# Row arithmetic and weight pieces move between GpSimd, VectorE and ACT in a two-block fp32 kernel

## The chip, the cores and the metric

The kernel runs on one core of one Trainium2 chip. The metric is the device time of one execution in microseconds (us). Its engines are TensorE (PE; PEld is its weight load), VectorE (DVE), ScalarE (ACT), GpSimd (POOL) and SyncE (SP), which issues most of the DMA loads.

## The reference, cut to what matters

The input is 256 tokens of width 1024. A first block (latent attention and retention side by side, then a feed-forward layer) is followed by a second (a hybrid of a delta rule and stick-breaking attention, then a mixture of 32 experts). All is fp32.

```python
# first block
h = x * (1.0 + sc1) + sh1                      # six modulation rows from c
proj = h @ w_in                                # latent attention + retention inputs
y = concat([mla(...), retention(...)]) @ w_out
x = layer_norm(ALPHA * x + gt1 * y, ln1_g, ln1_b)
h = x * (1.0 + sc2) + sh2
f = square(relu(h @ w_ff1)) @ w_ff2            # width 4096
x = layer_norm(ALPHA * x + gt2 * f, ln2_g, ln2_b)
# second block: 16 meta tokens in front, then
proj = x @ w_in                                # delta rule q, k, v; gates; attention q, k, v
dn_qkv = silu(causal_depthwise_conv(dn_qkv, conv_w))   # four taps
merged = gate0 * (o_dn @ w_branch_dn) + gate1 * (o_sb @ w_branch_sb)
x = layer_norm(ALPHA * x + merged @ w_out, ...)
x = layer_norm(ALPHA * x + moe(x), ...)        # router, then 32 experts
```

Where the text says residual rows, it means ALPHA * x with the layer norm's gain g and offset b of the layer before folded in: ALPHA * (x * g + b), two rows of 1024 numbers on all 128 partitions.

## The kernel before, in words

The 256 tokens are two tiles of 128 (xh[0] and xh[1], 128x1024 each). Weights come in slabs of 1 MB from SP's queue into a ring of three buffers (tile `raw`). A matrix product in fp32 is made of three products of rounded parts (`mm3`, L317 to L319): high by high, low by high, high by low. So each slab is cut in pieces of 128x1024 by `piece`: ACT casts the high part (`hi`, L299), then VectorE, or GpSimd where the caller says so, subtracts it from the slab to get the low part (`lo`, L300). A pair of buffers for such a piece is free again when TensorE has used it; there are four pairs, and one more (`wx`) until the feed-forward's end.

A list scheduler puts the instructions of each engine in order; `issue_after(x)` forbids it to put one ahead of x. Each engine then runs its own list in order, and semaphores join the lists.

The stages, in order of time: modulation and input projection; `first_mixers`, in which attention heads (`mla`) run interleaved with retention and with pieces of the modulation (`ada`); in it the softmax's scale is L654, its exponential L658, the next heads' q and k projections follow; `residuals` (L811 to L816) is a generator that loads two rows, lets ACT scale them by ALPHA, and lets GpSimd multiply and add them to both tiles; the output projection; `feed_forward`, whose loop of 16 turns computes f (L317 to L319, tile `f`), ffr (ACT, relu), ffs (DVE, the square, L894), its high and low parts ffh (L470) and ffl (L471), and one turn later the second product (tile `ff`). At its end `split` cuts four pieces of the second block's weights, the residual's sum (L874, L875) and the layer norm run per token tile, and a diagonal matrix of reciprocal deviations (L999) turns the normalized tile into fT. `delta_inputs` makes six projections `dn` of two blocks of 128 channels each, copies them (xp, ACT), applies four taps of the convolution (L1082 the first, L1084 the other three) and silu (L1085), and transposes the result (kT, vT). Then come the mixers, the router and the experts (`moe`), whose slabs stream in as the router's list of experts says (SP, L1917).

Of the kernel before, what the change touches and what calls it, by code (L numbers as in the profile page):

```python
# [44 lines left out]
SPLITS = 4  # L45
# [173 lines left out]
class Core:  # L219
# [70 lines left out]
    def piece(self, parts, t, i, size, pool):  # L290
# [5 lines left out]
        wp, bufs = (self.wx, 1) if self.wx and self.cuts % (SPLITS + 1) == 0 else (self.wp, SPLITS)  # L296
# [248 lines left out]
    def first_mixers(self, qc, krp, rr, sg, res):  # L545
# [52 lines left out]
        for i in range(NH // 2 + 2):  # L598
            for j in (i, i - 1, i - 2):
                if 0 <= j < NH // 2:  # L600
# [4 lines left out]
                    if i:  # L605
                        next(ret, None)
            if i == 1:
# [7 lines left out]
        with self.tc.issue_after(self.copied):  # L615
            next(res)
# [4 lines left out]
    def mla(self, i, uq, ukv, ch, cl, kr, vt):  # L621
# [13 lines left out]
        for j, (no, ro) in enumerate(((lo, hi), (hi, lo))):  # L635
# [3 lines left out]
            self.copied = nc.gpsimd.tensor_copy(kk[ro, j, :], kr[ro]).ins  # L639
# [22 lines left out]
        for j in range(2):  # L662
            for t, c in enumerate((slice(0, P), slice(P, 3 * P))):
                e = 2 * j + t
                nc.vector.tensor_scalar(p[:, j, c], p[:, j, c], r[:, e:e + 1], None, op0=ALU.mult)
# [141 lines left out]
    def residuals(self, row, xh, ring=None):  # L807
# [3 lines left out]
        nc.scalar.mul(g, g, ALPHA)  # L811
        nc.scalar.mul(b, b, ALPHA)
        yield
        for x in xh:
            nc.gpsimd.tensor_tensor(x, x, g, op=ALU.mult)
            nc.gpsimd.tensor_tensor(x, x, b, op=ALU.add)  # L816
        yield
# [59 lines left out]
    def feed_forward(self, gt2):  # L877
# [34 lines left out]
        for i in range(nf):  # L912
            last = first(i)
            if i == 2:
                res = self.xh
                for _ in self.residuals(2, res):
                    pass
# [15 lines left out]
        def split(after=None):  # L933
            i, j = next(cut)
            with self.tc.issue_after(after) if after else nullcontext():
                self.piece(parts[i], raw[i], j, 2048, True)
# [13 lines left out]
        split()  # L950
        for t in range(2):
# [10 lines left out]
            last = self.spread(rs[:, 0:1], res[t], s[:, 2:3])  # L962
            split(last)
            nc.vector.scalar_tensor_tensor(x2, x2, rs[:, 0:1], b2, op0=ALU.mult, op1=ALU.add, accum_out=s[:, 3:4])
            nc.vector.tensor_scalar(s[:, 4:5], s[:, 3:4], -1.0 / D, None, op0=ALU.mult)
            nc.vector.scalar_tensor_tensor(xh[t], x2, s[:, 4:5], ge, op0=ALU.add, op1=ALU.mult)
            self.spread(self.re[:, t:t + 1], x2, s[:, 4:5])
            diag[t], last = self.diagonal(self.re[:, t:t + 1])
            if t == 0:
                split(last)  # L970
# [85 lines left out]
    def delta_inputs(self, chains):  # L1056
# [10 lines left out]
        for i in range(6):  # L1067
            pd = [self.ps("dn") for _ in range(2)]
            for last in self.products(self.weights2(256 * i, (1,)), [p[:, :TM] for p in pd]):
# [7 lines left out]
            for b in range(2):  # L1077
# [4 lines left out]
                nc.vector.tensor_scalar(y, xp[:, b, :TM], tap(0), None, op0=ALU.mult)  # L1082
# [386 lines left out]
    def second_mixers(self):  # L1469
# [27 lines left out]
        for t in range(2):  # L1497
            r = self.small()[:, 0:1]
            nc.vector.tensor_scalar(r, self.re[:, t:t + 1], ALPHA, None, op0=ALU.mult)
            nc.scalar.mul(self.xh[t], self.xh[t], r)  # L1500
            nc.gpsimd.tensor_tensor(self.xh[t], self.xh[t], b, op=ALU.add)
# [58 lines left out]
    def mix_out(self):  # L1560
# [27 lines left out]
        def norm(t):  # L1588
            mean, r = self.stats(res[t], out=self.rs[:, 6 + t:7 + t])
            nc.vector.tensor_scalar(res[t], res[t], mean, r, op0=ALU.subtract, op1=ALU.mult)  # L1590

        between = {(1, 0, 3): [(turn, 0, 0)], (1, 1, 2): [(turn, 0, 1), (norm, 0)],
                   (1, 1, 3): [(logits, 0, 0), (logits, 0, 1), (self.choose, 0, pl[0]), (turn, 1, 0)]}
# [182 lines left out]
    def moe(self, xh, pl):  # L1776
# [6 lines left out]
        low(nc.gpsimd, 0, slice(0, D))  # L1783
# [376 lines left out]
```

## Time and profile before

| | before |
|---|---|
| time, median of 3 runs | 917.5 us (914.66 to 918.17) |
| the profiled execution | 914.81 us |
| its span, first to last instruction | 913.1 us |
| mean granted clock of TensorE | 0.957 |
| TensorE busy | 812.8 us, 89% |
| VectorE busy | 511.7 us, 56% |
| ACT busy | 310.4 us, 34% |
| GpSimd busy | 117.2 us, 13% |

Shares are means over stages that differ: a stage's own waits tell what a change in it is worth. In a row of the order of time the bracket gives how long the engine was idle ahead of the instruction and what ended that. A row with "x2" is two instructions that follow each other directly.

### The profile page before, as it was taken

Reading aid. Unit: us, or ns where it says so; the run is one execution under the profiler, and the core shown is the slowest. Engines: PE = TensorE matmul, PEld = TensorE weight load, DVE = VectorE, ACT = ScalarE, POOL = GpSimd, SP = SyncE. Lnnn points to the kernel's source line nnn. Section 1 sums busy time; section 2 is a strip of 40 time slices with the busy share of each in tenths; the row PEclk is TensorE's granted clock in tenths of the full one; section 3 lists DMA queues with packets and bytes.
Section 4 is the critical chain, followed back from the end, with each engine's and each line's share of the span. In section 5 each row is a group of like instructions: output and inputs, shape, how many; then the busy total and the mean of one; then the engine's idle time right before and its main releaser. Section 6 shows DMA issues by size and latency. Waiting matters only on the chain.

```text
span 913.1 us, 13514 instructions
## 1 busy us (share of the span) xinstructions
PE 812.8 (89%) x5311; PEld 611.3 (67%) x5311; DVE 511.7 (56%) x971; ACT 310.4 (34%) x491; POOL 117.2 (13%) x121
## 2 busy tenths in 40 slices
PE   4989789989999999889798999999988988866884
PEld 3886456668999998679797997899863443322321
DVE  4595748595655555845787458875655333120214
ACT  3343336354444444333463343544332211100101
POOL 0002400140000001452415201300010000000000
PEclk9999989989999999797999999999979999999987
DMA  8967546655755555033332130489655999999994
GB/s 310 365 230 299 209 185 253 232 192 180 254 185 189 185 192 193 24 127 136 136 139 84 42 108 13 145 339 335 264 229 244 421 414 421 421 421 421 422 416 179
DMA packets 35895, 218.10 MB, mean 239 GB/s; under 512 B 5976, under 2 KB 6496, under 8 KB 12144
## 3 DMA queue, kind: packets, MB, share of 16 engines
q1 hardware_dynamic: 33888, 215.09, 61.0%
q10 hardware_dynamic: 1936, 2.07, 0.8%
q8 instruction: 44, 0.72, 0.3%
q14 instruction: 27, 0.22, 0.1%
HBM read 216.09 MB, written 1.05 MB: 238 GB/s over the span
## 4 chain that ended last, share of the span: by engine, by line
PE 62%; DMA 17%; DVE 13%; ACT 4%; POOL 2%; issue 2%; SPq 0%; DVEq 0%; ACTq 0%; POOLq 0%
DMA expert<-in_w_down 8%; DMA raw<-in_w_gu 4%; PE gu L323 4%; PE ff L319 3%; PE ff L317 3%; PE ff L318 3%; PE f L319 3%; PE f L317 3%; PE f L318 3%; DMA expert<-in_w_gu 2%; PE dn L323 2%; PE Z L323 2%; PE xT L323 2%; PE y L318 2%; PE gate L317 2%
## 5 line engine op out<-in xcount | busy, mean ns | idle before, releaser
L300 DVE TENSOR_TENSOR lo<-raw,hi 128x1024 fp32r<-128x1024 f32 (+1 forms) x145 | 175.6, 1224 | 96.1 <-ACT hi L299 95.7
L299 ACT CAST hi<-raw 128x1024 fp32r<-128x1024 f32 (+1 forms) x155 | 156.6, 1028 | 176.7 <-PE ff L319 57.2
L323 PE MATMUL gu<-expert,xT 128*32 128x512 f32 (+1 forms) x424 | 81.4, 629 | 9.5 <-DMA expert<-in_w_gu 9.5
L317 PE MATMUL f<-hTh,hi 128*128 128x256 f32 x256 | 72.1, 282 | 0.0
L319 PE MATMUL f<-hTh,lo 128*128 128x256 f32 x256 | 71.8, 280 | 0.0
L318 PE MATMUL f<-hTl,hi 128*128 128x256 f32 x256 | 71.7, 280 | 0.0
L323 PEld LDWEIGHTS gu<-expert,xT 128*32 128x32 f32 (+1 forms) x424 | 20.0, 122 | 55.8 <-issue 36.4
L317 PE MATMUL ff<-hi,ffh 128*128 128x512 f32 x128 | 52.2, 408 | 4.4 <-DVE ffh L470 4.4
L323 PE MATMUL dn<-expert,aT 128*32 128x512 f32 (+1 forms) x224 | 46.9, 626 | 9.7 <-DMA expert<-in_w_down 9.7
L319 PE MATMUL ff<-hi,ffl 128*128 128x512 f32 x128 | 52.6, 411 | 2.0 <-DVE ffl L471 2.0
L318 PE MATMUL ff<-lo,ffh 128*128 128x512 f32 x128 | 52.2, 408 | 0.0
L318 PEld LDWEIGHTS f<-hTl,hi 128*128 128x128 f32 x256 | 48.2, 188 | 0.9 <-issue 0.2
L317 PEld LDWEIGHTS f<-hTh,hi 128*128 128x128 f32 x256 | 48.2, 188 | 0.9 <-issue 0.2
L319 PEld LDWEIGHTS f<-hTh,lo 128*128 128x128 f32 x256 | 48.3, 189 | 0.0
L2005 DVE TENSOR_TENSOR a<-gu,a 128x256 f32<-128x256 f32 x10 | 4.2, 422 | 72.8 <-ACT a L2004 72.8
L300 POOL TENSOR_TENSOR lo<-raw,hi 128x1024 fp32r<-128x1024 f32 x10 | 25.1, 2518 | 121.3 <-ACT hi L299 121.3
L323 PEld LDWEIGHTS dn<-expert,aT 128*32 128x32 f32 (+1 forms) x224 | 11.3, 121 | 39.4 <-issue 19.3
L317 PE MATMUL gate<-hTh,hi 128*128 128x256 f32 x128 | 37.4, 292 | 0.0
L2027 DVE SCALAR_TENSOR_TENSOR yl<-dn,s,yh 128x512 fp32r<-128x512 f32 x20 | 15.0, 749 | 38.8 <-ACT yh L2026 38.8
L323 PE MATMUL xT<-P,hTh 128*128 128x256 f32 x80 | 25.1, 339 | 12.7 <-ACT xT L1959 11.2
L319 PE MATMUL gate<-hTh,lo 128*128 128x256 f32 x128 | 36.1, 282 | 0.0
L318 PE MATMUL gate<-hTl,hi 128*128 128x256 f32 x128 | 36.0, 281 | 0.0
(597 smaller groups left out, 1981.0 us busy)
## 6 DMA issues: line engine op xcount, KB each, us to landing
expert<-in_w_gu SPq DMA_DIRECT2D x53, 1024.0 KB, 13.7
raw<-in_w_ff SPq DMA_DIRECT2D x32, 1024.0 KB, 4.8
expert<-in_w_down SPq DMA_DIRECT2D x24, 1024.0 KB, 19.7
raw<-in_w_in SPq DMA_DIRECT2D x22, 1024.0 KB, 4.8
raw<-in_w_gu SPq DMA_DIRECT2D x11, 1024.0 KB, 19.3
wa<-in_w_ada SPq DMA_DIRECT2D x8, 1024.0 KB, 8.7
raw<-in_w_gate SPq DMA_DIRECT2D x8, 1024.0 KB, 4.7
raw<-in_w_ada SPq DMA_DIRECT2D x8, 1024.0 KB, 4.8
```

The costliest lines, as they stand in the source:

```text
L299: nc.scalar.copy(h[:, :w], f)
L300: (nc.gpsimd if pool else nc.vector).tensor_tensor(l[:, :w], f, h[:, :w].bitcast(F32), op=ALU.subtract)
L317: mm(out, sh, mh, start=first, stop=False)
L318: mm(out, sh, ml, start=False, stop=False)
L319: return mm(out, sl, mh, start=False, stop=last)
L323: i = self.nc.tensor.matmul(out, lhsT, rhs, start=first, stop=last).ins
L2005: nc.vector.tensor_tensor(a, pg[:, FE:], a, op=ALU.mult)
L2027: nc.vector.scalar_tensor_tensor(yl, py, w[:, 0:1], yh.bitcast(F32), op0=ALU.mult, op1=ALU.subtract)
```

## The change

It has six parts:

1. `residuals` uses two VectorE instructions per tile (x * ALPHA * g, then b * ALPHA + x) in place of two ACT scalings and two GpSimd instructions per tile. In `first_mixers` they are taken one at a time in turns 1 to 4 of the loop; in `feed_forward` the rows are loaded in turn 1, and one instruction follows the f product of each of turns 2 to 5.
2. In `delta_inputs` the second piece of each slab has its low part cut by VectorE, and the first tap goes from VectorE to ACT.
3. The four low parts at the feed-forward's end go from GpSimd to VectorE, two behind the last ffl, two behind the first tile's normalization.
4. Behind the second block's mixers one VectorE instruction takes the place of ACT's multiply and GpSimd's add, for each tile.
5. In `moe` the low part of the first tile goes from GpSimd to VectorE, behind the first tile's choice of experts.
6. While `wx` is open, it has two pairs of buffers, so there are six pairs and not five.

```diff
-SPLITS = 4
+SPLITS, MORE_SPLITS = 4, 2
...
-        wp, bufs = (self.wx, 1) if self.wx and self.cuts % (SPLITS + 1) == 0 else (self.wp, SPLITS)
+        more = self.wx and self.cuts % (SPLITS + MORE_SPLITS) < MORE_SPLITS
+        wp, bufs = (self.wx, MORE_SPLITS) if more else (self.wp, SPLITS)
...
+            if 0 < i <= 4:
+                next(res)
...
-        with self.tc.issue_after(self.copied):
-            next(res)
...
         g, b = self.row(row, "rowg", ring), self.row(row + 1, "rowb", ring)
-        nc.scalar.mul(g, g, ALPHA)
-        nc.scalar.mul(b, b, ALPHA)
         yield
         for x in xh:
-            nc.gpsimd.tensor_tensor(x, x, g, op=ALU.mult)
-            nc.gpsimd.tensor_tensor(x, x, b, op=ALU.add)
-        yield
+            nc.vector.scalar_tensor_tensor(x, x, ALPHA, g, op0=ALU.mult, op1=ALU.mult)
+            yield
+            nc.vector.scalar_tensor_tensor(x, b, ALPHA, x, op0=ALU.mult, op1=ALU.add)
+            yield
...
-            if i == 2:
+            if i == 1:
                 res = self.xh
-                for _ in self.residuals(2, res):
-                    pass
+                rows = self.residuals(2, res)
+                next(rows)
+            if 1 < i < 6:
+                with self.tc.issue_after(last):
+                    next(rows)
...
-                self.piece(parts[i], raw[i], j, 2048, True)
+                self.piece(parts[i], raw[i], j, 2048, False)
...
-        split()
+        for _ in range(2):
+            split(last)
...
-            last = self.spread(rs[:, 0:1], res[t], s[:, 2:3])
-            split(last)
+            self.spread(rs[:, 0:1], res[t], s[:, 2:3])
...
-            nc.vector.scalar_tensor_tensor(xh[t], x2, s[:, 4:5], ge, op0=ALU.add, op1=ALU.mult)
+            last = nc.vector.scalar_tensor_tensor(xh[t], x2, s[:, 4:5], ge, op0=ALU.add, op1=ALU.mult).ins
...
             if t == 0:
-                split(last)
+                for _ in range(2):
+                    split(last)
...
-            for last in self.products(self.weights2(256 * i, (1,)), [p[:, :TM] for p in pd]):
+            for last in self.products(self.weights2(256 * i), [p[:, :TM] for p in pd]):
...
-                nc.vector.tensor_scalar(y, xp[:, b, :TM], tap(0), None, op0=ALU.mult)
+                nc.scalar.mul(y, xp[:, b, :TM], tap(0))
...
-            nc.scalar.mul(self.xh[t], self.xh[t], r)
-            nc.gpsimd.tensor_tensor(self.xh[t], self.xh[t], b, op=ALU.add)
+            nc.vector.scalar_tensor_tensor(self.xh[t], self.xh[t], r, b, op0=ALU.mult, op1=ALU.add)
...
-        low(nc.gpsimd, 0, slice(0, D))
+        with self.tc.issue_after(self.last):
+            low(nc.vector, 0, slice(0, D))
```

What it does to the order is shown at three places. On VectorE in attention, ahead of the scale of the latent queries (`s` from `ss`), the list before was:

```order
L300 TENSOR_TENSOR lo_836<-raw_833,hi_835 128x1024
L300 TENSOR_TENSOR lo_840<-raw_833,hi_839 128x1024
L300 TENSOR_TENSOR lo_846<-raw_843,hi_845 128x1024
L578 TENSOR_SCALAR s_119_858<-ss_851 128x2 x2
L582 TENSOR_TENSOR rmsd_862<-ident,s_119_858 128x512
```

The same place after, where xh_100 and xh_101 are the two token tiles:

```order
L301 TENSOR_TENSOR lo_838<-raw_831,hi_837 128x1024
L301 TENSOR_TENSOR lo_844<-raw_841,hi_843 128x1024
L814 SCALAR_TENSOR_TENSOR xh_100<-xh_100,rowg_750 128x1024
L814 SCALAR_TENSOR_TENSOR xh_101<-xh_101,rowg_750 128x1024
L816 SCALAR_TENSOR_TENSOR xh_100<-rowb_752,xh_100 128x1024
L816 SCALAR_TENSOR_TENSOR xh_101<-rowb_752,xh_101 128x1024
L579 TENSOR_SCALAR s_119_856<-ss_849 128x2 x2
L583 TENSOR_TENSOR rmsd_860<-ident,s_119_856 128x512
```

Four instructions of 128x1024 now stand between the last low part and the scale. On ACT at the feed-forward's end, before (hi is a cast of a piece, sq the square of a token tile):

```order
L299 CAST hi_3246<-raw_3240 128x1024
L299 CAST hi_3272<-raw_3258 128x1024
L892 ACTIVATE ffr_3222<-f_460_3173 128x512
L372 ACTIVATE sq_3312,s_488_3311<-xh_100,s_483_3300 128x1024
L299 CAST hi_3316<-raw_3258 128x1024
L299 CAST hi_3330<-raw_3260 128x1024
L372 ACTIVATE sq_3324,s_491_3323<-x_3308,s_483_3300 128x1024
```

And after:

```order
L300 CAST hi_3268<-raw_3254 128x1024
L300 CAST hi_3272<-raw_3254 128x1024
L892 ACTIVATE ffr_3218<-f_460_3169 128x512
L300 CAST hi_3326<-raw_3256 128x1024
L300 CAST hi_3330<-raw_3256 128x1024
L373 ACTIVATE sq_3312,s_489_3311<-xh_100,s_484_3300 128x1024
L300 CAST hi_3574<-raw_3572 128x1024
L300 CAST hi_3578<-raw_3572 128x1024
L373 ACTIVATE sq_3320,s_491_3319<-x_3308,s_484_3300 128x1024
```

One more cast stands ahead of the last ffr, and two casts ahead of the first square, where none stood; the two that follow (from raw_3572) are the first slab of the delta branch. On VectorE in `delta_inputs`, before (y are the taps' sums):

```order
L1082 TENSOR_SCALAR y_3731<-xp_3728,cols 128x272
L1084 SCALAR_TENSOR_TENSOR y_3731<-xp_3728,cols,y_3731 128x272 x3
L300 TENSOR_TENSOR lo_3825<-raw_3822,hi_3824 128x1024
L1082 TENSOR_SCALAR y_3738<-xp_3728,cols 128x272
L1084 SCALAR_TENSOR_TENSOR y_3738<-xp_3728,cols,y_3738 128x272 x3
```

And after:

```order
L301 TENSOR_TENSOR lo_3821<-raw_3818,hi_3820 128x1024
L301 TENSOR_TENSOR lo_3825<-raw_3818,hi_3824 128x1024
L1088 SCALAR_TENSOR_TENSOR y_3734<-xp_3724,cols,y_3734 128x272 x3
L1088 SCALAR_TENSOR_TENSOR y_3803<-xp_3800,cols,y_3803 128x272 x3
L301 TENSOR_TENSOR lo_3897<-raw_3894,hi_3896 128x1024
```

A turn now has two low parts and six taps on VectorE, and no first tap.

## Rows read from the trace of the kernel before

**Rows 1.** Page, section 1, and the rate line of section 2.

```profile
PE 812.8 (89%) x5311; PEld 611.3 (67%) x5311; DVE 511.7 (56%) x971; ACT 310.4 (34%) x491; POOL 117.2 (13%) x121
...
GB/s 310 365 230 299 209 185 253 232 192 180 254 185 189 185 192 193 24 127 136 136 139 84 42 108 13 145 339 335 264 229 244 421 414 421 421 421 421 422 416 179
```

**Rows 2.** Waits of PE: us in total, times, longest us.

```profile
PE q L317 <- ACT p L658: 6.6, 1, 6.6
...
PE vT L331 <- ACT y L1085: 4.9, 2, 3.3
PE ff L317 <- DVE ffh L470: 4.4, 2, 2.5
...
PE dn L319 <- POOL lo L300: 3.0, 1, 3.0
PE ff L319 <- DVE ffl L471: 2.0, 1, 2.0
PE sbv L319 <- DVE s L965: 1.5, 1, 1.5
```

**Rows 3.** Page, costliest groups: low parts cut by DVE and by POOL.

```profile
L300 DVE TENSOR_TENSOR lo<-raw,hi 128x1024 fp32r<-128x1024 f32 (+1 forms) x145 | 175.6, 1224 | 96.1 <-ACT hi L299 95.7
...
L300 POOL TENSOR_TENSOR lo<-raw,hi 128x1024 fp32r<-128x1024 f32 x10 | 25.1, 2518 | 121.3 <-ACT hi L299 121.3
```

**Rows 4.** Order of time, attention: start us, us, engine, line, operation, [idle before].

```profile
75.65 1.06 ACT L812 ACTIVATE rowb<-rowb 128x1024 f32<-128x1024 f32 x1
75.78 1.23 DVE L300 TENSOR_TENSOR lo<-raw,hi 128x1024 fp32r<-128x1024 f32 x1 [1.40 <-ACT hi L299]
...
81.45 0.23 DVE L578 TENSOR_SCALAR s<-ss 128x2 f32<-128x2 f32 x2 [4.45 <-PE ss L323]
...
104.89 9.48 DVE L654 TENSOR_SCALAR s<-s 128x4 f32<-128x4 f32 x1
...
109.72 4.63 POOL L816 TENSOR_TENSOR xh<-xh,rowb 128x1024 f32<-128x1024 f32 x2
...
116.18 0.58 PE L317 MATMUL q<-cnh,hi 128*128 128x256 f32 x1 [6.61 <-ACT p L658]
```

**Rows 5.** Stretches: length, busy by engine (count), then PEclk, DMA share, GB/s.

```profile
116.00:122.00 6.00, 5.82 (x28) 4.55 (x28) 2.49 (x8) 3.43 (x10) 0.00 (x0) 0.55 0.01 4
198.00:208.00 10.00, 7.40 (x20) 5.61 (x21) 8.25 (x8) 0.00 (x0) 2.84 (x3) 0.66 0.32 105
...
408.00:416.00 8.00, 7.00 (x34) 7.00 (x35) 2.62 (x5) 2.20 (x3) 3.27 (x2) 0.57 0.68 262
...
434.00:440.00 6.00, 6.00 (x50) 6.00 (x50) 5.31 (x7) 3.42 (x6) 3.60 (x4) 1.00 0.40 162
```

**Rows 6.** Order of time, DVE at the feed-forward's start.

```profile
193.11 2.89 DVE L894 TENSOR_TENSOR ffs<-ffr 128x512 f32<-128x512 f32 x1
```

**Rows 7.** Order of time, the feed-forward's end and the embedding.

```profile
361.60 1.06 ACT L299 CAST hi<-raw 128x1024 fp32r<-128x1024 f32 x1 [0.37 <-PE f L318]
...
372.73 1.15 ACT L372 ACTIVATE sq<-xh,s 128x1024 bf16<-128x1024 f32 x1 [9.58 <-DVE s L958]
...
381.58 3.78 PE L323 MATMUL fT<-diag,xh 128*128 128x128 f32 x16 [1.43 <-POOL diag L999]
...
395.47 1.95 PE L323 MATMUL fT<-diag,xh 128*128 128x128 f32 x16
```

**Rows 8.** Order of time, delta inputs.

```profile
428.94 0.81 POOL L1191 COPY km<-y 128x16 f32<-128x16 f32 x1 [5.34 <-PE dn L319]
...
437.79 2.32 DVE L1082 TENSOR_SCALAR y<-xp,cols 128x272 f32<-128x272 f32 x1 [0.59 <-ACT xp L1078]
440.14 1.58 DVE L1084 SCALAR_TENSOR_TENSOR y<-xp,cols,y 128x272 f32<-128x272 f32 x3
441.64 0.35 DVE L1082 TENSOR_SCALAR y<-xp,cols 128x272 f32<-128x272 f32 x1
```

**Rows 9.** Order of time, SP's queue, the first load after the router.

```profile
693.15 3.32 SPq L1917 DMA_DIRECT2D expert<-in_w_gu  x6
```

More of the change, by code (lines that the diff above doesn't have):

```diff
@@ L638, in mla @@
             nc.scalar.copy(kk[no, j, :], pk[no, :T])
-            self.copied = nc.gpsimd.tensor_copy(kk[ro, j, :], kr[ro]).ins
+            nc.gpsimd.tensor_copy(kk[ro, j, :], kr[ro])
         yield
@@ L664, in mla @@
                 e = 2 * j + t
-                nc.vector.tensor_scalar(p[:, j, c], p[:, j, c], r[:, e:e + 1], None, op0=ALU.mult)
+                self.normed = nc.vector.tensor_scalar(p[:, j, c], p[:, j, c], r[:, e:e + 1], None, op0=ALU.mult).ins
         yield
@@ L961, in feed_forward @@
             rs = self.small()
-            last = self.spread(rs[:, 0:1], res[t], s[:, 2:3])
-            split(last)
+            self.spread(rs[:, 0:1], res[t], s[:, 2:3])
             nc.vector.scalar_tensor_tensor(x2, x2, rs[:, 0:1], b2, op0=ALU.mult, op1=ALU.add, accum_out=s[:, 3:4])
             nc.vector.tensor_scalar(s[:, 4:5], s[:, 3:4], -1.0 / D, None, op0=ALU.mult)
-            nc.vector.scalar_tensor_tensor(xh[t], x2, s[:, 4:5], ge, op0=ALU.add, op1=ALU.mult)
+            last = nc.vector.scalar_tensor_tensor(xh[t], x2, s[:, 4:5], ge, op0=ALU.add, op1=ALU.mult).ins
             self.spread(self.re[:, t:t + 1], x2, s[:, 4:5])
-            diag[t], last = self.diagonal(self.re[:, t:t + 1])
+            diag[t], _ = self.diagonal(self.re[:, t:t + 1])
             if t == 0:
-                split(last)
+                for _ in range(2):
+                    split(last)
         self.xh = xh
@@ L1590, in norm, with chosen @@
             nc.vector.tensor_scalar(res[t], res[t], mean, r, op0=ALU.subtract, op1=ALU.mult)
+        def chosen():
+            self.last = self.choose(0, pl[0])
         between = {(1, 0, 3): [(turn, 0, 0)], (1, 1, 2): [(turn, 0, 1), (norm, 0)],
-                   (1, 1, 3): [(logits, 0, 0), (logits, 0, 1), (self.choose, 0, pl[0]), (turn, 1, 0)]}
+                   (1, 1, 3): [(logits, 0, 0), (logits, 0, 1), (chosen,), (turn, 1, 0)]}
         for t in range(2):
```

## The prediction, made before the changed kernel had run

> **What bounds the kernel now.** I read the engine shares first, then the rates of the DMA by slice, then TensorE's waits sorted by what ended them, then the stretches around those waits in order of time, with the granted clock. The reader is to see a kernel with two halves. TensorE is busy for 89% of the span, and GpSimd for only 13%. From the 32nd of the 40 slices on the DMA runs at 414 to 422 GB/s, slice after slice [rows 1]: this is the stream of the experts' weights. It starts again with the load at 693.15, once the router's result is known [rows 9], and its length is fixed by its bytes. So whatever is gained ahead of 693 moves the whole tail forward, and nothing that is gained inside the tail counts. The change touches only work ahead of it.
>
> GpSimd's 13% are dearer than they look. Among TensorE's waits stand q on the softmax (6.6 us), vT on the convolution's output (4.9), ff on its high and low parts (4.4 and 2.0), dn on a low part cut by GpSimd (3.0) and sbv (1.5) [rows 2], 22.4 us in all. Behind nearly all of them is the same picture: a short VectorE instruction that ends when a long GpSimd instruction beside it ends. A VectorE TENSOR_SCALAR on 128x4 began at 104.89 and took 9.48 us, to 114.37; the GpSimd pairs of the residual ran beside it, and the last of them ended at 114.35 [rows 4]. VectorE cuts a low part in 1.22 us on the mean, GpSimd the same in 2.52 [rows 3]. After each such wait TensorE also runs for some us at or near the lower of its two levels (0.5 is 1.2 GHz, 1 is 2.4): the granted clock is 0.55 in 116 to 122 and 0.66 in 198 to 208 [rows 5].
>
> The profiled execution took 914.8 us around a span of 913.1; the median of the runs is 917.5 and the fastest 914.7. I make the sum against 914.8.
>
> **The change, stage by stage.**
>
> *Residual rows in attention.* The two GpSimd pairs go (the second took 4.63 us, both some 9.3). VectorE gets four instructions of 128x1024 instead, in the new order directly behind a low part that ended at 77.0 (75.78 + 1.23) and ahead of the scale that began at 81.45, after an idle time of 4.45 us [rows 4]. The nearest row for one of them is that low part, 1.23 us: four are 4.9, so the scale starts at 81.9 and not at 81.45, a cost of 0.5. The rows they read have landed by then: ACT scaled the later of them at 75.65. The gain: the softmax is ready up to 9.3 us sooner, and TensorE, which had run dry at 109.57 (116.18 - 6.61), needs only 6.6 of them. The slow clock behind it goes as well: 5.82 busy us at 0.55 lose 2.6. Together 6.6 + 2.6 - 0.5 = 8.7; I take **8**, with bounds of 4 (the next chain in line, rotary and scores, is late) and 9.
>
> *Residual rows at the start of the feed-forward.* The same pairs stretched ffs (2.89 us at 193.11 [rows 6]; a 128x1024 instruction needs only 1.22), ffh and ffl. Two of the waits of [rows 2] are this place: 2.5 of the 4.4, and 2.0. The clock of 198 to 208 loses 7.40 x 0.34 = 2.5 [rows 5]. Sum 7.0. In the new order the four new instructions come later, one in each of four turns of the loop, behind ffl, where only the next slab's low part waits. I take **6.5**, bounds 3 and 7.
>
> *End of the feed-forward and embedding.* Here I expect little, against the look of the rows. The remaining 1.9 of ff's wait comes from one GpSimd low part and would go, but in ACT's new order two casts stand ahead of ffr where there was one, and the first can't start before TensorE leaves the buffers (ACT's cast at 361.60 [rows 7]). One cast more is 1.05 us, so about 1 us of the 1.9 comes back. Then two further casts stand ahead of the first square, which began at 372.73; their buffers come free only in the middle of the last ff block. So the chain square, power, diagonal, fT starts no earlier than before, though TensorE gets there sooner: I let it wait 2 to 3 us where it waited 1.43 at 381.58. For the second token tile, VectorE's two new low parts stand inside the chain. From the end of the residual's sum at about 383.3 that chain is five VectorE instructions of 1.2 us (two of them the low parts), three half ones, and a square, two powers and a diagonal with their handovers, some 2.5 us: about 10, so that the second fT starts at about 393.5 instead of 395.47 [rows 7]. Less 1 us of slow clock behind the waits: **1**, with bounds of -2 and 5 (all of 1.9 + 1.4 + 1.5).
>
> *First projection of the delta branch.* The wait of 3.0 on GpSimd's low part goes, since by the new order both parts of this slab are cut on VectorE ahead of the second fT. The clock of 408 to 416 loses 7.00 x 0.43 = 3.0 [rows 5]. I take **5.5**, bounds 3 and 6.
>
> *The other five projections.* VectorE set the pace. A turn is one first tap stretched to 2.32, three taps 1.58, one first tap 0.35, three taps 1.58 [rows 8] and one low part 1.22, together 7.05 us and the handovers. New: two low parts and six taps, 2.44 + 3.16 = 5.6. TensorE's 48 matmuls of a turn take 48 x 0.12 = 5.8 (50 in 6.00 us in 434 to 440 [rows 5]). So TensorE sets the pace again, narrowly. ACT gets two multiplications more a turn; the nearest row, a cast of 128x1024 in 1.06 [rows 7], bounds each from above, and it has room for that. The last turn's chain to vT (copy, tap on ACT, taps, silu) can't be hidden, and I leave 1.4 of the 4.9 us there: **3.5**, bounds 0 and 6 (4.9 and a clock dip behind it).
>
> *What is worth nothing.* The one instruction in place of a multiply and an add behind the mixers: TensorE is busy there. The router's low part goes from GpSimd to VectorE; it stretched one small instruction by about 1 us, and its own 1.22 now stands in the same chain: 0, bounds -1 and 1. The sixth pair of piece buffers has no price of its own except ACT's order above.
>
> Sum: 8 + 6.5 + 1 + 5.5 + 3.5 = 24.5, so 890.3 against 914.8. Low bounds add up to 7, high ones to 34; not all fall the same way.
>
> **The rivals.**
>
> *All of it comes back.* Every wait and every slow stretch goes and the embedding gains too: about 33 us, 882. Against it speaks ACT's new order.
>
> *VectorE blocks GpSimd in turn.* GpSimd's small instructions remain in chains: powers and diagonals in the embedding, copies of y. One copy took 0.81 us at 428.94, while VectorE cut a low part [rows 8]. Six such steps stand in the embedding's two chains and several behind; at up to 1.2 us each for six, some 7 us are lost: 897. The Trainium skill ("SBUF — State Buffer", Who interferes with whom) says that a VectorE instruction with two SBUF inputs and a GpSimd one that reads SBUF exclude each other for the whole instruction, and that the order of issue decides who waits. By that rule the change swaps the victim. The 9.48 us of [rows 4] agree with the first half.
>
> *VectorE becomes the bound.* The other projections and the embedding run at VectorE's pace (5.6 against 5.8 us is a thin margin) and give nothing or -2, and the first projection only its wait: 8 + 6.5 - 2 + 3 = 15.5 at most, with a later chain in attention about 13: 901.
>
> *ffr late in every turn of the feed-forward: slower.* With six buffers, both casts of a turn wait for the buffers of the f block just ended, and in ACT's new order they stand ahead of ffr. The chain is two casts 2.1, the second low part 1.22, then ffs and ffh at about half a low part each: ffh is ready some 4.5 us behind f's end. It is covered by one ff block, 24 matmuls of 512 columns, about 5.4 us (an estimate by columns from the 0.12 above). If the chain is over 0.9 us longer than that, each of 14 turns pays. From 1.8 us a turn (a chain of 7.2 us) the whole gain is gone; at 2.3, 922. For it: the cover is thin. Against it: ACT has nothing else to do at that point, and a cast's own time is 1.06 in [rows 7].
>
> *The change doesn't reach the waits.* The waits that were put down to GpSimd were due to another thing, a late weight for instance: 914. Against it: four VectorE instructions in different stages end with GpSimd's.
>
> **How the numbers follow.** My forecast, 890.3, has 0.57; all back (882) 0.12; VectorE blocks GpSimd (897) 0.13; VectorE the bound (901) 0.09; not reached (914) 0.04; slower (922) 0.05. The range goes from 880 to 902 and leaves the last two out. Half a per cent, about what a measurement can tell here, is 4.6 us: faster 0.91, same 0.04, slower 0.05. Since the runs' median lies above the profiled one, I say 891.
>
> **What would show it.** In the changed profile: the attention's 128x4 TENSOR_SCALAR below 0.5 us and no TensorE gap of 6 us after it; ffs near 0.7 us at the first ff block, with the clock at 1; vT's wait below 2.5 us; no wait of dn on a low part; the experts' loads starting near 669 instead of 693. The forecast is wrong if q waits for another chain, if a wait of ff on ffh appears in every turn, or if fT waits over 4 us in the embedding.

## The result, and the profile after

The changed kernel took 884.7 us (median of 4 runs, 882.2 to 890.2) beside 916.1 (914.5 to 918.2) for the kernel before on the same chip: a ratio of 0.967, interval 0.963 to 0.971. The profiled execution took 882.2 us around a span of 880.5, where that of before had 914.8 around 913.1, so the span shrank by 32.6. The forecast was 891 with a range of 880 to 902. Sign and range were right; the gain was a third larger than the sum said.

The page of the kernel after, section 1 and the rate line of section 2, beside [rows 1]:

```profile
PE 799.9 (91%) x5311; PEld 601.1 (68%) x5311; DVE 497.3 (56%) x980; ACT 309.9 (35%) x497; POOL 66.5 (8%) x100
...
GB/s 320 332 227 317 162 351 258 211 275 193 258 191 191 191 192 144 47 175 167 121 96 60 86 60 53 256 325 364 144 222 380 421 421 421 420 421 421 421 417 175
```

VectorE took over work, and yet its busy time fell, from 511.7 to 497.3: in the kernel before it counted as busy while it was held up. TensorE's busy time fell by 13 at the same number of instructions, most of it clock: the mean granted clock rose from 0.957 to 0.975. TensorE's waits after (us in total, times, longest), beside [rows 2]:

```profile
PE fT L324 <- POOL diag L1003: 3.4, 2, 3.0
...
PE s L324 <- DVE pT L676: 2.2, 1, 2.2
...
PE dm L324 <- DVE s L1132: 1.5, 1, 1.5
```

The waits of q, of ff on its two parts, of dn on a low part and of sbv are gone; that of vT is down to 0.2. New are `s` on the transposed softmax (2.2) and `dm`, a short step in the delta rule's decays (1.5). The load after the router, on SP's queue, starts 32 us sooner than in [rows 9]:

```profile
661.08 3.31 SPq L1924 DMA_DIRECT2D expert<-in_w_gu  x6
```

Where the time came from can be read by putting the same matmul of both traces side by side: the shift of its start, medians over all matmuls of a stretch, and the difference of two stretches is what the stage between them gained. In us (positive is faster than before; the last column is the shift at the mixers, summed from the start):

| kernel | start | attention, output projection | feed-forward start | its end, embedding | first projection | other five | shift at the mixers |
|---|---|---|---|---|---|---|---|
| forecast | 0 | 8 | 6.5 | 1 | 5.5 | 3.5 | 24.5 |
| after | -1.9 | 9.9 | 7.5 | 3.4 | 9.1 | 3.5 | 31.5 |
| after_again | -3.3 | 10.0 | 7.5 | 3.4 | 9.1 | 3.5 | 30.2 |
| rows_alone | 0.3 | 11.5 | 7.6 | 0.1 | 0.1 | -0.7 | 18.9 |
| end_alone | -0.3 | -0.3 | -0.6 | 4.3 | 9.1 | -1.1 | 11.1 |
| delta_alone | -1.9 | 0.1 | 0.1 | 0.0 | 7.5 | 2.7 | 8.5 |
| rows_back | -0.5 | 0.0 | -0.6 | 3.4 | 7.5 | 1.6 | 11.4 |
| delta_back | -1.8 | 11.5 | 7.5 | 4.3 | 9.1 | -1.0 | 29.6 |
| tap_back | -0.1 | 9.9 | 7.5 | 3.4 | 6.0 | 2.4 | 29.1 |
| five_pairs | -0.7 | 10.0 | 7.6 | 4.8 | 4.9 | 3.6 | 30.2 |
| low_behind_sum | -1.8 | 9.9 | 7.6 | 5.4 | 7.5 | 1.5 | 30.1 |
| five_behind_sum | -0.7 | 9.9 | 7.6 | 6.6 | 6.5 | 1.6 | 31.5 |
| beside_read | -1.7 | 0.5 | 7.5 | 3.4 | 6.0 | 2.8 | 18.5 |
| beside_write | -1.8 | 9.3 | 7.5 | 3.4 | 9.1 | 3.5 | 31.0 |

The first column is work that the change doesn't touch (modulation and input projection); it differs by 3.6 between kernels that are alike there, so single profiles are compared by stage and not by their ends. Where attention has 11.5 and not 9.9, a slow stretch in the output projection is missing too (clock 1.00 in 160 to 180 in rows_alone, 0.90 and 0.93 in the kernel after). Behind the mixers the kernel after gains 1.1 more. That can't be credited to parts 4 and 5, which were not run by themselves: from the mixers to the experts' loads it gains 0.6, and rows_alone, which lacks these parts, gains 0.8.

### The profile page after: what moved, and what is told of

Same layout as the page of the kernel before. It is cut to its first block, busy times and chain, and to the rows that moved or that the text cites. A ratio compares the mean times of both kernels' runs of the same rounds, so it can differ in the third digit from the quotient of the medians.

```text
span 880.5 us, 13495 instructions
## 1 busy us (share of the span) xinstructions
PE 799.9 (91%) x5311; PEld 601.1 (68%) x5311; DVE 497.3 (56%) x980; ACT 309.9 (35%) x497; POOL 66.5 (8%) x100
## 4 chain that ended last, share of the span: by engine, by line
PE 66%; DMA 16%; DVE 10%; ACT 3%; POOL 2%; issue 2%; SPq 0%; DVEq 0%; POOLq 0%; ACTq 0%
DMA expert<-in_w_down 8%; DMA raw<-in_w_gu 4%; PE gu L324 4%; PE f L320 3%; PE f L318 3%; PE f L319 3%; PE ff L318 3%; PE ff L320 3%; PE ff L319 3%; DMA expert<-in_w_gu 2%; PE dn L324 2%; PE Z L324 2%; PE xT L324 2%; PE y L319 2%; PE fT L324 2%; PE y L320 2%
## 5 line engine op out<-in xcount | busy, mean ns | idle before, releaser
L301 DVE TENSOR_TENSOR lo<-raw,hi 128x1024 fp32r<-128x1024 f32 (+1 forms) x155 | 185.7, 1212 | 85.5 <-ACT hi L300 85.1
L324 PE MATMUL gu<-expert,xT 128*32 128x512 f32 (+1 forms) x424 | 79.6, 620 | 10.3 <-DMA expert<-in_w_gu 10.3
L324 PE MATMUL dn<-expert,aT 128*32 128x512 f32 (+1 forms) x224 | 51.4, 672 | 7.1 <-DMA expert<-in_w_down 7.0
L320 PE MATMUL ff<-hi,ffl 128*128 128x512 f32 x128 | 50.7, 396 | 0.0
L2034 DVE SCALAR_TENSOR_TENSOR yl<-dn,s,yh 128x512 fp32r<-128x512 f32 x20 | 15.0, 749 | 40.3 <-ACT yh L2033 40.2
L324 PE MATMUL xT<-P,hTh 128*128 128x256 f32 x80 | 24.9, 335 | 13.6 <-ACT xT L1966 11.1
L2011 ACT ACTIVATE a<-gu 128x256 f32<-128x256 f32 x10 | 3.8, 384 | 85.9 <-PE gu L324 85.9
```

The costliest lines, as they stand in the source:

```text
L301: (nc.gpsimd if pool else nc.vector).tensor_tensor(l[:, :w], f, h[:, :w].bitcast(F32), op=ALU.subtract)
L320: return mm(out, sl, mh, start=False, stop=last)
L324: i = self.nc.tensor.matmul(out, lhsT, rhs, start=first, stop=last).ins
L2011: nc.scalar.activation(a, pg[:, :FE], AF.Silu)
L2034: nc.vector.scalar_tensor_tensor(yl, py, w[:, 0:1], yh.bitcast(F32), op0=ALU.mult, op1=ALU.subtract)
```

## The stages after, in rows

Attention, VectorE in order of time (start us, us, engine, line, operation, idle before), beside [rows 4]:

```profile
76.79 2.35 DVE L814 SCALAR_TENSOR_TENSOR xh<-xh,rowg 128x1024 f32<-128x1024 f32 x2
79.06 2.35 DVE L816 SCALAR_TENSOR_TENSOR xh<-rowb,xh 128x1024 f32<-128x1024 f32 x2
83.36 0.23 DVE L579 TENSOR_SCALAR s<-ss 128x2 f32<-128x2 f32 x2 [1.94 <-PE ss L324]
...
107.97 0.17 DVE L655 TENSOR_SCALAR s<-s 128x4 f32<-128x4 f32 x1
```

The softmax's scale, the same instruction that took 9.48 us, takes 0.17. The four new instructions end at 81.4, and the scale of the latents still waits 1.94 for TensorE: they cost nothing. On TensorE's side, the first q behind the softmax, then the stage between two matmuls that both kernels have, first before, then after (columns as in [rows 5]):

```profile
117.19 0.36 PE L318 MATMUL q<-cnh,hi 128*128 128x256 f32 x1
```

```profile
100.00:159.97 59.97, 51.56 (x297) 32.75 (x296) 43.66 (x94) 23.94 (x63) 12.06 (x8) 0.94 0.61 233
```

```profile
101.90:151.98 50.08, 47.51 (x297) 30.38 (x296) 34.74 (x94) 24.00 (x63) 2.76 (x4) 1.00 0.80 294
```

The stage is 9.9 us shorter at the same 297 matmuls. TensorE's idle time in it falls from 8.4 to 2.6 us, and most of what is left is the new wait of `s`, at 128.59. q starts no sooner than before (116.18): TensorE's order changed with the rows, and from 104 us on matmuls of the retention (rs, ro) stand ahead of it. Then the feed-forward's start, beside [rows 6], and the two stretches of [rows 5] with their clock (the third number from the end):

```profile
188.76 0.69 DVE L894 TENSOR_TENSOR ffs<-ffr 128x512 f32<-128x512 f32 x1 [0.31 <-ACT ffr L892]
...
190.84 0.42 DVE L471 CAST ffh<-ffs 128x512 fp32r<-128x512 f32 x1
...
192.31 0.68 DVE L472 TENSOR_TENSOR ffl<-ffs,ffh 128x512 fp32r<-128x512 f32 x1
```

```profile
116.00:122.00 6.00, 5.86 (x46) 4.16 (x43) 3.59 (x16) 1.84 (x5) 1.35 (x2) 1.00 0.95 355
...
198.00:208.00 10.00, 10.00 (x64) 8.92 (x63) 7.67 (x8) 4.42 (x5) 0.00 (x0) 1.00 0.52 204
```

All three are at their plain length, and TensorE is at 1.00 in both stretches. At the feed-forward's end ACT and VectorE do this:

```profile
346.07 1.06 ACT L300 CAST hi<-raw 128x1024 fp32r<-128x1024 f32 x1 [0.37 <-PE f L319]
347.02 0.59 ACT L892 ACTIVATE ffr<-f 128x512 f32<-128x512 f32 x1
...
347.64 0.69 DVE L894 TENSOR_TENSOR ffs<-ffr 128x512 f32<-128x512 f32 x1 [0.90 <-ACT ffr L892]
348.37 0.43 DVE L471 CAST ffh<-ffs 128x512 fp32r<-128x512 f32 x1
```

Of the two casts ahead of the last ffr only one falls behind the end of f; ffh is ready at 348.8, TensorE does not wait for it, and its clock is 1.00 through 344 to 354. In the embedding, VectorE, GpSimd and TensorE:

```profile
361.99 0.15 DVE L374 TENSOR_SCALAR s<-s 128x1 f32<-128x1 f32 x1
362.06 1.22 DVE L301 TENSOR_TENSOR lo<-raw,hi 128x1024 fp32r<-128x1024 f32 x1
...
362.22 1.46 POOL L375 TENSOR_TENSOR rs<-s,mhalf 128x1 f32<-128x1 f32 x1 [4.11 <-DVE s L374]
...
364.21 3.79 PE L324 MATMUL fT<-diag,xh 128*128 128x128 f32 x16 [3.00 <-POOL diag L1003]
```

GpSimd's power on 128x1 takes 1.46 us here and 0.54 where VectorE is idle beside it (357.56). It ends 0.4 behind the low part that VectorE cuts: now GpSimd is the one held up, for 0.9 us, in the chain on which fT waits. In the delta branch, stretches of the kernel after (as in [rows 5]), and then the two stretches of the kernel before that follow the one in [rows 5]:

```profile
408.00:416.00 8.00, 8.00 (x68) 7.99 (x67) 7.13 (x11) 6.23 (x13) 0.98 (x3) 1.00 0.40 133
```

```profile
416.00:424.00 8.00, 8.00 (x49) 8.00 (x48) 2.70 (x9) 2.59 (x5) 2.85 (x4) 0.65 0.27 94
424.00:432.00 8.00, 8.00 (x61) 8.00 (x61) 4.83 (x6) 3.21 (x5) 2.78 (x2) 0.92 0.10 39
```

After, TensorE is busy throughout at 1.00, VectorE for 7.13 of 8.00: TensorE sets the pace, by the thin margin that was forecast. Before, a second slow stretch followed the one of [rows 5]; 8.00 x 0.35 + 8.00 x 0.08 = 3.4 us lie there.

## Experiments

**The residual rows alone (rows_alone).** The kernel before with part 1 of the change. (Parts 4 and 5 were not run by themselves.)

```diff
...
-            nc.gpsimd.tensor_tensor(x, x, g, op=ALU.mult)
-            nc.gpsimd.tensor_tensor(x, x, b, op=ALU.add)
...
+            nc.vector.scalar_tensor_tensor(x, x, ALPHA, g, op0=ALU.mult, op1=ALU.mult)
+            yield
+            nc.vector.scalar_tensor_tensor(x, b, ALPHA, x, op0=ALU.mult, op1=ALU.add)
+            yield
...
```

> The kernel before with the residual rows alone moved to VectorE. Theory (GpSimd's long instructions stretch VectorE's beside them, each place for itself): the shift of TensorE's matmuls in the changed kernel was 9.9 us in attention and 7.5 us at the feed-forward's start, so this part alone gives 17 us, a ratio near 0.981. Rival (the parts work together, since a free stretch keeps the clock up for later ones): clearly more than 20 us, or the delta branch moves too although nothing of it is changed.

Measured: 895.3 us beside 915.7, ratio 0.977 (0.974 to 0.980), a gain of 20.4, where 17 had been expected; 1.6 of the difference is the slow stretch in the output projection, which is missing here. TensorE's waits in this kernel:

```profile
PE vT L331 <- ACT y L1087: 4.9, 2, 3.3
...
PE dn L319 <- POOL lo L300: 2.9, 1, 2.9
...
PE ff L317 <- DVE ffh L470: 1.9, 1, 1.9
```

The wait of q and 4.5 of the 6.4 of ff are gone, and everything behind the feed-forward stands as before. The table has the whole gain in attention, the output projection and at the feed-forward's start, and a loss of 0.7 at the other five projections.

**The feed-forward's end alone (end_alone).** The kernel before with parts 3 and 6: the sixth pair, and the four low parts on VectorE.

```diff
...
-                self.piece(parts[i], raw[i], j, 2048, True)
+                self.piece(parts[i], raw[i], j, 2048, False)
...
-        split()
+        for _ in range(2):
+            split(last)
...
```

> The kernel before with the sixth pair of buffers and the four low parts at the feed-forward's end alone moved. Theory: 3.4 us at the last ff block and nothing in the embedding, 3 to 4 us in all, ratio near 0.996. Rival (as I had forecast: the cast ahead of ffr and the low parts in the chain take it back): 1 us, no change.

Measured: 904.6 beside 915.7, ratio 0.988 (0.985 to 0.991), a gain of 11.1, far more than expected. Only 4.3 of it lie in the stage that was edited. Another 9.1 are in the first projection of the delta branch, whose second low parts are still cut by GpSimd here; the other stages lose 2.3. GpSimd in order of time, this kernel first, then the kernel before:

```profile
380.90 2.35 POOL L301 TENSOR_TENSOR lo<-raw,hi 128x1024 fp32r<-128x1024 f32 x1
...
398.68 6.04 POOL L1028 TENSOR_TENSOR f<-hTh,hTl 128x512 f32<-128x512 f32 x4 [4.96 <-PE sbv L320]
```

```profile
399.07 7.50 POOL L1026 TENSOR_TENSOR f<-hTh,hTl 128x512 f32<-128x512 f32 x4
...
406.61 4.66 POOL L300 TENSOR_TENSOR lo<-raw,hi 128x1024 fp32r<-128x1024 f32 x2
```

And ACT's first casts of the delta branch's pieces, again this kernel first:

```profile
373.98 1.98 ACT L300 CAST hi<-raw 128x1024 fp32r<-128x1024 f32 x2
```

```profile
400.11 1.05 ACT L299 CAST hi<-raw 128x1024 fp32r<-128x1024 f32 x1 [2.07 <-PE sbv L319]
```

Before, the high parts were cast only from 400.1 on, once TensorE had freed a pair of buffers; by then GpSimd had begun the sums `f`, and the low part came behind them, at 406.6. GpSimd itself had been idle from 393.1 to 398.5, so the four low parts of the feed-forward's end were not what held this one up. Here ACT casts the slab at 373.98, GpSimd cuts its low part at 380.9, ahead of `f`, and the wait of dn does not arise. By these rows it is the sixth pair of buffers that gives the 9.1; the sixth pair was not run alone.

**The delta branch alone (delta_alone).** The kernel before with part 2.

```diff
-            for last in self.products(self.weights2(256 * i, (1,)), [p[:, :TM] for p in pd]):
+            for last in self.products(self.weights2(256 * i), [p[:, :TM] for p in pd]):
...
-                nc.vector.tensor_scalar(y, xp[:, b, :TM], tap(0), None, op0=ALU.mult)
+                nc.scalar.mul(y, xp[:, b, :TM], tap(0))
```

> The kernel before with the low parts and the first tap of the delta projections alone moved. Theory: 9.1 us at the first projection and 3.5 us at the others, 12 to 13 us together, ratio near 0.986; the slow clock at 418 to 426, which I had not counted, goes with this part. Rival (that slow clock went because the stages ahead of it had changed): 9 us, and the clock still falls behind the first projection.

Measured: 907.0 beside 915.7, ratio 0.991 (0.987 to 0.994), a gain of 8.7, where 12 to 13 had been expected. The projections gain 13 by the matmuls of 452 to 461, but then some of it is given back. A wait on the decays appears, and the clock behind it falls:

```profile
463.38 0.39 PE L323 MATMUL dm<-s,cst 64*64 64x1 f32 x4 [1.55 <-DVE s L1128]
```

```profile
464.00:468.00 4.00, 4.00 (x22) 3.93 (x22) 2.64 (x9) 1.79 (x5) 0.81 (x1) 0.57 0.20 41
```

TensorE now comes to the decays sooner than they are ready. The kernel after has the same wait of 1.5 (above), with its clock still at 1.00.

**The residual rows put back (rows_back).** The kernel after with part 1 undone (the diff of rows_alone, reversed).

> The changed kernel with the residual rows back on GpSimd and ACT. Theory: 17 us slower than the changed kernel, some 14 us faster than before, ratio near 0.985, and the 9 us TENSOR_SCALAR and the waits of q and ff are back. Rival (the parts work together): the sum of the parts misses the whole by more than 4 us.

Measured: 904.1 beside 915.7, ratio 0.987 (0.984 to 0.990): 19.4 more than the 884.7 of the kernel after. The waits that had gone are back:

```profile
PE q L318 <- ACT p L659: 6.6, 1, 6.6
...
PE ff L320 <- DVE ffl L472: 5.3, 1, 5.3
```

Taken alone the three parts gain 20.4, 11.1 and 8.7, together 40.2, and the change gains 31.4. The 9 us too many are the first projection: end_alone and delta_alone both contain it, since either way of cutting that low part sooner removes the wait.

**The delta branch put back (delta_back).** The kernel after with part 2 undone.

> The changed kernel with the delta projections as they were: second low parts on GpSimd, first tap on VectorE. New theory (rows and end give 31 us by themselves, and the delta part's 6 us at the projections are given back at the decay chain behind them): the same time as the changed kernel within 3 us, ratio 0.966 to 0.970, vT waits some 2 us, and dm not at all. Rival (the sum of the stages as predicted): the 9 us of the delta part are lost, ratio 0.975.

Measured: 888.1 beside 916.4, ratio 0.971 (0.967 to 0.975), some 3.4 slower than the kernel after, with intervals that overlap. The first projection keeps its full 9.1; the other five lose 1.0 where they gained 3.5, with vT waiting again:

```profile
PE vT L332 <- ACT y L1089: 4.5, 3, 1.9
```

So beside the other parts, part 2 is worth only the other five projections, 4.5 us there.

**The first tap put back on VectorE (tap_back).** The kernel after, but for one line.

```diff
-                nc.scalar.mul(y, xp[:, b, :TM], tap(0))
+                nc.vector.tensor_scalar(y, xp[:, b, :TM], tap(0), None, op0=ALU.mult)
```

> The changed kernel with the first tap back on VectorE and the low parts left there. Theory (the tap on ACT is needed, since VectorE otherwise has 2.44 + 3.16 + 0.71 = 6.3 us a turn against TensorE's 5.8): vT waits 2 to 3 us, the decay chain's wait of 1.5 us goes; within 2 us of the changed kernel. Rival (moving the low parts alone does it): no wait of vT over 1 us.

Measured: 884.9 beside 916.4, ratio 0.965 (0.961 to 0.968), the same as the kernel after. vT waits 0.6 and not the 2 to 3 expected: VectorE has 6.3 us a turn by the prediction's way of adding and TensorE 5.8, and yet VectorE does not set the pace. The decays' wait is gone, as expected. The other five projections keep 2.4 of their 3.5. The first one has 6.0 and not 9.1, by the clock, of which more below.

**Five pairs instead of six (five_pairs).**

```diff
-SPLITS, MORE_SPLITS = 4, 2
+SPLITS, MORE_SPLITS = 4, 1
```

> The changed kernel with five pairs of piece buffers and not six; the first slab of the delta branch is then cast behind the second fT again, and no cast stands ahead of the first square. New theory (the 9 us at the first projection come from the sixth pair, which lets its pieces be cut before the matmuls need them, whoever cuts them): the first projection waits for a low part again, 4 to 8 us of its 9 come back, and the embedding's first fT waits less than the 3.0 us it now does; in all some 4 us slower than the changed kernel, ratio 0.970. Rival (they come from VectorE cutting the low parts): as fast as the changed kernel, no wait of dn.

Measured: 882.8 beside 916.4, ratio 0.963 (0.959 to 0.966), the same within the intervals, where some 4 us slower had been expected. dn waits 0.5 on a low part, fT 2.0 instead of 3.0. So where VectorE cuts the low parts, dn's wait is all but gone without the sixth pair too (delta_alone, with five pairs, has none). What five pairs gain in the embedding (4.8 against 3.4) they lose, and more, in the first projection (4.9 against 9.1), mostly by the clock.

**The last two low parts behind the second tile's sum (low_behind_sum).** The kernel after, with the two low parts that stood behind the first tile's normalization moved behind the second tile's residual sum.

```diff
-                self.gated(res[t], n, acc[t][nh], gt2, s[:, nh:nh + 1])
+                last = self.gated(res[t], n, acc[t][nh], gt2, s[:, nh:nh + 1])
+            if t:
+                for _ in range(2):
+                    split(last)
...
-            if t == 0:
-                for _ in range(2):
-                    split(last)
```

> The changed kernel with the last two low parts at the feed-forward's end put behind the second tile's residual sum, out of the first tile's chain square, power, diagonal. Theory (fT's wait of 3.0 us in the changed kernel is this chain, lengthened by a low part ahead of the variance and by one beside GpSimd's power, 1.46 us): the wait falls to about 1.5 us, some 1.5 us faster in the embedding with a smaller slow stretch behind it, 1 to 3 us in all. Rival (the chain starts late because of the two casts ahead of the first square): the wait stays at 2.5 us or more.

Measured: 884.4 beside 916.4, ratio 0.964 (0.961 to 0.967). TensorE's wait:

```profile
PE fT L324 <- POOL diag L1003: 1.5, 2, 0.9
```

The longest wait falls from 3.0 to 0.9 and the embedding gains 2.0 more: the two low parts stood in that chain. In the kernel after the first of them ran on VectorE ahead of the variance (at 360.86), and the second, of 362.06, stretched GpSimd's power, which takes 0.54 here. The first projection and the wait on the decays took the gain back.

**Both of these (five_behind_sum).** low_behind_sum with five pairs.

> The changed kernel with five pairs of buffers and the last two low parts behind the second tile's residual sum. Theory (the embedding's chain bounds fT; five pairs leave no cast ahead of the first square, and the low parts leave the chain): fT waits less than 1 us, 1 to 3 us faster than the changed kernel, before a possible slow stretch at the projections. Rival (the slow stretch behind the delta branch's small matmuls, which some runs show and some not, moves the time more than this): within 2 us of the changed kernel.

Measured: 884.0 beside 916.2, ratio 0.965 (0.961 to 0.969). The end and the embedding gain 3.2 more than in the kernel after; the first projection and the decays take 4.5 back.

**The kernel after once more (after_again).** No edit.

> The changed kernel itself, on the same chip as the version above, so that a difference of 2 us between them can be told. Theory (the slow stretch at the projections, 388 to 400, and the one at 20 to 27 come by chance): its shifts against the first profile differ by 2 to 4 us at these places and nowhere else. Rival (they belong to the kernel): the same clock in every stretch as in the first profile.

Measured: 883.9 beside 916.2, ratio 0.965 (0.962 to 0.968). Every stage behind the start repeats to 0.1 us, its clock in the first projection too. No kernel here beats the changed one by more than the intervals.

**GpSimd reading beside attention, on rows that nobody needs (beside_read).** To tell contention from any dependence, the kernel after was given four GpSimd multiplications of 128x1024 where the old ones stood. They work on the row buffers after their last use, so nothing reads what they write: work is added and nothing waits for it.

```diff
...
+        if row == 0:
+            for _ in range(4):
+                nc.gpsimd.tensor_tensor(g, g, b, op=ALU.mult)
```

> The changed kernel with four GpSimd multiplications of 128x1024 added where the residual's stood before, but on two rows that nothing reads any more. No data waits for them. Theory (a GpSimd instruction that reads SBUF holds up VectorE's beside it, whatever it computes): the 128x4 TENSOR_SCALAR of the softmax is stretched to 5 to 10 us again, q waits some 6 us, the kernel is some 8 us slower than the changed one. Rival (in the kernel before, VectorE or ACT waited for the residual's data): no wait, the same time.

Measured: one execution of 895.4, some 11 above the kernel after. VectorE, GpSimd and TensorE in order of time, and a stretch:

```profile
106.61 2.56 DVE L658 TENSOR_SCALAR s<-s 128x4 f32<-128x4 f32 x1
...
111.17 3.33 DVE L669 TENSOR_SCALAR p<-p,s 128x128 f32<-128x128 f32 x4
114.42 0.54 DVE L679 COPY pT<-pt 128x384 f32<-128x384 f32 x1
...
106.80 9.91 POOL L823 TENSOR_TENSOR rowg<-rowg,rowb 128x1024 f32<-128x1024 f32 x4
...
115.02 0.39 PE L318 MATMUL kn<-cnh,hi 128*128 128x256 f32 x1 [2.12 <-DVE pT L679]
```

```profile
116.00:122.00 6.00, 6.00 (x29) 2.60 (x28) 0.64 (x2) 1.84 (x5) 0.71 (x1) 0.72 0.73 272
```

The two TENSOR_SCALARs end within 0.3 us of an end of a GpSimd instruction (at 109.3 and 114.2, four of 2.48 from 106.80 on); without GpSimd they take 0.17 and 1.01. Nobody waits for GpSimd's data here, so this stretching is contention and not dependence. The first one is held for 2.56 us and not for the 5 to 10 expected, and q, which was to wait for 6, does not wait. The copy that reads pt from PSUM runs at its plain 0.54. Behind the second one TensorE waits 2.12, and then its clock is 0.72 (6.00 x 0.28 = 1.7 us): 3.8 us follow from the stretching.

Of the 9.9 us that attention and output projection had gained 0.5 is left, so 9.4 are lost, and not all of that is contention. 3.2 of them lie in the output projection, where TensorE is busy throughout at a clock of 0.73 and 0.76 (170 to 180, 180 to 190). And the scheduler changed TensorE's order: up to 123 us it is that of the kernel before, without the retention's matmuls ahead of q. What the order alone costs was not run.

**GpSimd writing only (beside_write).** Eight memsets of the same row in place of the four multiplications; the scheduler put them a little later.

```diff
...
+        if row == 0:
+            for _ in range(8):
+                nc.gpsimd.memset(g, 0.0)
```

> The changed kernel with eight GpSimd memsets of 128x1024 in the same place: they write SBUF and read nothing. Theory by the Trainium skill (SBUF — State Buffer, Who interferes with whom: an instruction with two SBUF inputs contends with GpSimd's reads, not with its writes): instructions with two inputs keep their time (0.41 to 0.69 us for those of 128x512 and below); those with one input might still be held. Rival (any GpSimd instruction of some us stretches all of VectorE's): stretches of 1 us or more on two-input instructions beside the memsets.

Measured: one execution of 883.8, as the kernel after. GpSimd and VectorE in order of time:

```profile
120.29 8.44 POOL L823 MEMSET rowg<- 128x1024 f32 x8
...
123.68 1.23 DVE L750 TENSOR_TENSOR rr<-rr,sg 128x1024 f32<-128x1024 f32 x1 [0.63 <-ACT rr L748]
...
126.07 1.21 DVE L472 TENSOR_TENSOR mTr<-rr,mTr 128x1024 fp32r<-128x1024 f32 x1
...
127.85 0.91 DVE L658 TENSOR_SCALAR s<-s 128x4 f32<-128x4 f32 x1
```

For 8.4 us GpSimd writes, and VectorE's two-input instructions of 128x1024 take 1.23 and 1.21, as without it. One TENSOR_SCALAR is held until the last memset's end (0.91 instead of 0.17). Attention keeps 9.3 of its 9.9. So the instructions with two inputs pay for GpSimd's reading and not for its writing. For a TENSOR_SCALAR with one input, the kind that took 9.48 us, this does not follow: a memset holds it too, here only for what was left of the last one.

## Why the prediction was right, and where its sizes were off

**The mechanism.** The step "a short VectorE instruction that ends when a long GpSimd instruction beside it ends" is shown: in rows_alone and rows_back some 20 us come and go with the rows alone, and in beside_read GpSimd instructions whose results nobody needs stretch the same VectorE instructions and bring back a wait and a slow clock (3.8 us). The rival that the change doesn't reach the waits falls with it.

**Attention: 8 forecast, 9.9 measured.** The 0.5 for the four new instructions was no cost: behind them VectorE still waits for TensorE. The high bound of 9 was too low by 0.9. The wait and the clock of the sum make 9.2, but that this comes so near is partly luck: the sum had no term for the new wait of 2.2, nor for TensorE's new order. By the stretches above less idle time gave 5.8; the clock gave the 2.6 of the sum, and 1.4 is busy time that got shorter, which I did not trace.

**Feed-forward start: 6.5 forecast, 7.5 measured.** The sum was 7.0 and I had taken off half a microsecond without a row for it.

**Feed-forward end and embedding: 1 forecast, 3.4 measured.** The mis-sized step is ACT's order. I let a second cast come back behind f's end; only one was behind it, ffh was in time, and the whole wait of 1.9 went, with the slow clock after it: by the shifts the end gains 3.4 and the embedding nothing. In the embedding the step was right: fT waits 3.0, as forecast (2 to 3), and what is lost there is what sbv's wait gives back.

**First projection: 5.5 forecast, 9.1 measured.** This is the largest miss. I read the stretch of 408 to 416 and stopped; the slow stretch behind it, 3.4 us, belonged to the sum: 3.0 + 3.0 + 3.4 = 9.4. The cause was also told too narrowly. I credited VectorE's cutting in `delta_inputs` and gave the sixth pair no price beyond ACT's order; but either removes the wait. With five pairs and VectorE cutting it is gone (delta_alone) or 0.5 (five_pairs); with six pairs and GpSimd still cutting it is gone as well, with the full 9.1 (end_alone, delta_back); with five pairs and GpSimd it stands (before, rows_alone). Part 3 goes with the sixth pair in end_alone and delta_back, so that these two were told apart by ACT's casts alone.

**Other five projections: 3.5 forecast, 3.5 measured, for another reason.** They gain 5.5 by the matmuls of 452 to 461 and give back 2.0 at the decays. "A stall that goes shows what is late next" was not followed here: the decays' wait of 1.5 was in no term. That 3.5 was met is luck.

**Mixers, router, end: 0 forecast, 1.1 measured.** The load after the router starts at 661.1; the forecast had near 669, and the 8 us between are the terms above, less the slower start.

**The rivals.** *All of it comes back* (882) is nearer in number than the forecast, though the embedding, which it needed, gained nothing. *VectorE blocks GpSimd in turn* is real and small: 0.9 us at 362.22, once more at 370.67, where I had priced six steps. The Trainium skill ("SBUF — State Buffer", Who interferes with whom) says that a VectorE instruction with two SBUF inputs excludes a GpSimd one that reads SBUF, and not one that only writes it, while a tensor_scalar in a two-port mode can contend with either. The rows agree on each: 1.46 against 0.54 on GpSimd's power; 1.23 and 1.21 beside the memsets; 0.91 against 0.17 for the TENSOR_SCALAR there, though no row tells its mode. The 9.48 us that the prediction set beside the rule for two inputs are of a TENSOR_SCALAR with one; the row for two is ffs, 2.89 against 0.69. *VectorE becomes the bound* falls (7.13 of 8.00 busy), and *ffr late in every turn* too: no wait of ff is left in any turn.

## What to carry to other kernels

An engine that is idle 87% of the time can be the dearest one: add up what a long GpSimd instruction with SBUF inputs does to the VectorE instructions beside it, by comparing the same instruction's length with and without it, and follow that to TensorE's wait and to the clock behind the wait. When a wait is to go, sum the clock until it stands at 1.00 again, over the next narrow matmuls too, and ask for each end of the chain what else would remove it: two parts that both remove one wait don't add up. A pair of buffers can be such a part: here it let ACT cast a slab some 26 us sooner. A reordering that gains in one stage is worth only what the next chain (here the decays) lets through.

## What the runs showed of the hardware that was not expected

**The clock behind the same narrow matmuls.** Behind the 32 matmuls `ba` of 8 columns each in the first projection the clock falls in some kernels and not in others. From 4 us ahead of the first one, 16 us in two stretches, the kernel after first, then five_pairs:

```profile
387.20:395.20 8.00, 8.00 (x69) 8.00 (x68) 5.10 (x10) 5.32 (x8) 2.89 (x3) 1.00 0.39 131
395.20:403.20 8.00, 8.00 (x66) 8.00 (x65) 6.08 (x10) 4.48 (x8) 2.27 (x3) 1.00 0.36 133
```

```profile
385.40:393.40 8.00, 8.00 (x63) 8.00 (x62) 4.71 (x8) 5.32 (x8) 0.20 (x1) 0.89 0.70 262
393.40:401.40 8.00, 8.00 (x46) 8.00 (x47) 3.31 (x8) 1.59 (x3) 0.00 (x0) 0.69 0.37 133
```

TensorE is busy all the time in both. The long fall (0.55, 0.50, 0.50, 0.74 in stretches of 2 us, which loses 3.4 us) stands in before, rows_alone, five_pairs, tap_back and beside_read; a short one (two stretches of 0.5 to 0.7) in delta_alone, rows_back, low_behind_sum and five_behind_sum; none in after, after_again, end_alone, delta_back and beside_write. It is more than what lies between the medians of the five kernels near 884 us (882.8 to 884.9). The two profiles of the changed kernel agree, but the order of the instructions does not decide it: from 160 us on beside_read has the order of the kernel after on every engine, and here is its second stretch:

```profile
404.40:412.40 8.00, 8.00 (x44) 8.00 (x45) 3.41 (x8) 1.69 (x3) 0.07 (x1) 0.65 0.38 133
```

What does decide it stays open.

**How long VectorE is held.** In [rows 4] the TENSOR_SCALAR was held through four GpSimd instructions, 9.48 us; in beside_read, at the same place beside four of about the same length, only through the first, 2.56 (2.3 us each there, 2.5 here). The four in beside_read each need the one before; the old ones alternated between two tiles. Whether that is the reason wasn't tried.
